# A tuned two-layer hybrid transformer kernel in float32r: 64 bytes of padding behind each of three activation buffers, and 32 bytes ahead of the low weight parts

## The chip, the cores and the metric

The kernel runs on one core of one Trainium2 chip. The metric is the device time of one execution in microseconds. The profile is that of one execution, taken by the hardware profiler; the times beside it are of executions without it.

## The reference, cut to what matters

Two layers over 512 positions of width 1024 are computed in float32: a causal attention with forget gates (16 heads of 64) and a latent attention (16 heads, keys of 128 + 64, values of 128), each followed by a feed-forward block with a causal convolution of width 3, and a last norm.

```python
def conv_ffn(h, w_in, conv_w, conv_b, w_out):
    s_len = h.shape[1]
    u = h @ w_in                                    # 1024 -> 2 x 2816
    up = jnp.pad(u, ((0, 0), (CONV_W - 1, 0), (0, 0)))
    u = conv_b + sum(up[:, j:j + s_len] * conv_w[j] for j in range(CONV_W))
    gate, val = jnp.split(u, 2, axis=-1)
    return (jax.nn.silu(gate) * val) @ w_out        # 2816 -> 1024

def reference(x, ...):
    for layer in range(2):
        if layer < 1:
            x = x + fox_mixer(rmsnorm(x, fox_norm[layer]), ...)
        else:
            k_nope, k_rope, v = mla_shared_kv(x, ...)
            x = x + mla_mixer(rmsnorm(x, mla_norm[0]), ..., k_nope, k_rope, v, cos, sin)
        x = x + conv_ffn(rmsnorm(x, ffn_norm[layer]), ...)
    return rmsnorm(x, final_norm)
```

## The kernel before, in words

Everything is kept transposed: 128 features on the partitions, the 512 positions along the row. To keep float32 accuracy, every operand of a product is split into a high part (rounded to float32r) and a low part (the rest). One product of a weight tile with an activation tile is then three matmuls, written in `mm3`: high weight with high activation (L84), high weight with low activation (L85), low weight with high activation (L86). The weight is the stationary operand of 128 columns, the activation the moving operand of 512 columns. TensorE issues a weight load for every matmul, three per tile of the contraction.

Weights come by one DMA from SP's queue into `raw` (three buffers of 4 KB per partition). `load_w` then lets ScalarE copy them, rounded, into `whi` (L105) and lets VectorE, or POOL in the attention stages, subtract that from `raw` into `wlo` (L106); `whi` and `wlo` have two buffers of 4 KB each.

Activations lie in tiles of the tag `big`: 8 feature tiles, each with 512 high and 512 low values, 32 KB per partition, with three buffers that rotate through the program. `xraw`, `xn`, `oT`, `xs`, `act0`, `act1`, `lat`, the values `V` of the first attention and `qc` of the second all are such tiles. The last 6 feature tiles of the feed-forward's 22 are in `act2`, which lies in the feed-forward's own pool.

In the value projection of the first attention (`mm_v`, L416 to L418) the roles are turned: the activation is the stationary operand, the weight the moving one, with 272, 384 and 384 columns in three passes; one weight tile holds two feature rows `kk`, so that for the first pass row 1 starts 1088 bytes behind row 0. The attention stages have small loops of scores, softmax on ScalarE and VectorE, transposes, and values. In the feed-forward block, `evacuate` multiplies the sum by a norm factor, applies the convolution (L292, L294) and the gate, and splits the result into `act0` to `act2`. Of L294's operands, `c[:, s:]` begins one or two elements into its row.

The pools are laid out one behind the other in each partition, in the order in which they are opened and their tags are first used: small things, `xT` and the four scratch rows `r2`, then `raw`, `whi`, `wlo`, then the three `big`, and behind them the pool of the stage at hand (`fx`, `ffn0`, `ml`, `ffn1`, which share that space in turn). The order of the work is that of the program text; Tile adds the waits.

```python
def mm3(out, w, x, start, stop):
    (wh, wl), (xh, xl) = w, x
    pe.matmul(out, wh, xh, start=start, stop=False)
    pe.matmul(out, wh, xl, start=False, stop=False)
    pe.matmul(out, wl, xh, start=False, stop=stop)
```

Of the kernel before, what the change touches and what calls it, by code (L numbers as in the profile page):

```python
# [7 lines left out]
F32 = mybir.dt.float32  # L8
F32R = mybir.dt.float32r
# [6 lines left out]
P = 128  # L16
S = 512
NT = S // P
# [3 lines left out]
FH, FD = 16, 64  # L22
MH, MN, MR, MV = 16, 128, 64, 128
KVL, QL = 256, 768
KQ = QL // P
KL = KVL // P
# [8 lines left out]
G_FOX, G_FFN, G_KVIN, G_MLA, G_KV, G_Q, G_FIN, G_N = 0, 8, 24, 32, 40, 42, 48, 56  # L35
C_ID, C_MF, C_MM, C_COS, C_SIN, C_U, C_N = 0, 128, 640, 1152, 1664, 2176, 2688
R2 = 4
VCH = (0, 384, 768, 1040)

FOX_FILL = {12: (4, (0,) * 4), 13: ((0, 0, 1, 1), (1,) * 4), 14: ((0, 1, 2, 2), (2,) * 4), 15: ((2,), (3,) * 7)}  # L40
# [6 lines left out]
def tile_kernel(ctx, tc, xT_d, gains_d, bf_d, const_d, conv_d, wv_d, wq_d, wk_d, wfo_d,  # L47
                wdq_d, wdkv_d, wuqn_d, wuqr_d, wuk_d, wuv_d, wmo_d, wfi_d, wfu_d, out_d):
    nc = tc.nc
    v, a, g, pe = nc.vector, nc.scalar, nc.gpsimd, nc.tensor  # L50
# [4 lines left out]
    wp = ctx.enter_context(tc.tile_pool(name="wp", bufs=2))  # L55
    bp = ctx.enter_context(tc.tile_pool(name="bp", bufs=3))
    ps = ctx.enter_context(tc.tile_pool(name="ps", bufs=3, space=PSUM))
    dp = ctx.enter_context(tc.tile_pool(name="dp", bufs=1, space=DRAM))

    cnt = [0]  # L60

    def T(pool, shape, dt, tag, bufs=None):
        cnt[0] += 1
        kw = {} if bufs is None else {"bufs": bufs}
        return pool.tile(shape, dt, tag=tag, name=f"{tag}_{cnt[0]}", **kw)
# [7 lines left out]
    def r2():  # L73
        return T(cp, [P, 512], F32, "r2", R2)

    def big(k, name):
        return T(bp, [P, 8, 2, S], F32R, "big", 3)[:, :k]

    def f(ap):
        return ap.bitcast(F32)  # L80
# [7 lines left out]
    def load_w(src, shape, gain=None, eng=None, into=None, pieces=1):  # L88

        n = 1  # L90
        for s in shape[1:]:
            n *= s
        raw = T(wp, [P, 1024], F32, "raw", 3)[:, :n]
        cuts = [slice(i * n // pieces, (i + 1) * n // pieces) for i in range(pieces)]
        for c in cuts:
            nc.sync.dma_start(raw[:, c], src[:, c])
        if gain is not None:
            k, c = gain
            r3 = raw.rearrange("p (k c) -> p k c", c=n // k)
            g.tensor_tensor(out=r3, in0=r3, in1=c.unsqueeze(2).to_broadcast([P, k, n // k]), op=ALU.mult)  # L100
        if into is None:
            into = T(wp, [P, 1024], F32R, "whi", 2), T(wp, [P, 1024], F32R, "wlo", 2)
        hi, lo = (t[:, :n] for t in into)
        for c in cuts:
            a.copy(hi[:, c], raw[:, c])  # L105
            (eng or v).tensor_tensor(out=lo[:, c], in0=raw[:, c], in1=f(hi[:, c]), op=ALU.subtract)  # L106
        names = " ".join(f"d{i}" for i in range(len(shape) - 1))
        kw = {f"d{i}": shape[i + 1] for i in range(len(shape) - 1)}
        pat = f"p ({names}) -> p {names}"
        return hi.rearrange(pat, **kw), lo.rearrange(pat, **kw)  # L110
# [51 lines left out]
    def bcast_ps(r, m=NT):  # L162
# [6 lines left out]
        for j, part in enumerate((f(rh), rl)):  # L169
            d = T(cp, [P, 512], F32R, "r2", R2)[:, :m * P]  # L170
            for i in range(m):
# [74 lines left out]
    def out_proj(tile_of, gbase):  # L246

        xs = big(KD, "xs")
        squares = Squares()
        for d in range(KD):  # L250
            pt, steps = tile_of(d)
            for _ in steps:
                pass
            v.tensor_tensor(out=xT[:, d, :], in0=pt, in1=xT[:, d, :], op=ALU.add)  # L254
            split_x(xs, d, xT[:, d, :], None if gbase is None else gain(gbase, d))
            squares.add(xT[:, d, :], a if d == KD - 1 else g)
        return xs, squares
# [21 lines left out]
    def ffn(layer, xs, squares, gbase):  # L279
        with tc.tile_pool(name=f"ffn{layer}", bufs=1, reuse_waits="tile") as fp:  # L280
            conv = T(fp, [P, 192], F32, "conv", 1)[:, :KF * 8].rearrange("p (j b c) -> p j b c", b=2, c=4)
            nc.gpsimd.dma_start(conv, conv_d[layer])
            act = [big(8, "act0"), big(8, "act1"), T(fp, [P, KF - 16, 2, S], F32R, "act2", 1)]
            rstd = Rstd(squares)
            cs = {}
# [16 lines left out]
            for j in range(KF):  # L302
                for b in range(2):
                    wh, wl = load_w(wfi_d[layer, j, b], [P, KD, P])
                    pt = acc()
                    for k in range(KD):
                        mm3(pt, (wh[:, k, :], wl[:, k, :]), parts(xs, k), k == 0, k == KD - 1)
                    rstd.after(lambda R, j=j, b=b, pt=pt: evacuate(j, b, pt, R))
# [3 lines left out]
            def load(d, c):  # L312
                k0, kn = chunks[c]
                return load_w(wfu_d[layer, d, :, k0 * P:(k0 + kn) * P], [P, kn, P])
# [76 lines left out]
    with tc.tile_pool(name="fx", bufs=1, reuse_waits="tile") as fp:  # L391
        mask = T(fp, [P, S], F32, "mask", 1)
        bfb = T(fp, [P, 64], F32, "bfb", 1)[:, :FH]
        nc.gpsimd.dma_start(bfb, bf_d)
        xraw = big(KD, "xraw")
        V = T(bp, [P, NT, FH, 2 * FD], F32R, "big", 3)
        squares = Squares()

        def load_v(c, kp):
            if c == 2:  # L400
                nc.sync.dma_start(xT[:, 2 * kp, :], xT_d[2 * kp])
            w = load_w(wv_d[c][kp], [P, 2, VCH[c + 1] - VCH[c]], pieces=2 if (c, kp) == (2, 0) else 1)
            if c == 2:
                nc.sync.dma_start(xT[:, 2 * kp + 1, :], xT_d[2 * kp + 1])
            return w

        def mm_v(c, kp, w, pts):
            n = VCH[c + 1] - VCH[c]
            for kk in range(2):
                k = 2 * kp + kk  # L410
                if c == 2:
                    split_x(xraw, k, xT[:, k, :], gain(G_FOX, k))
                for t in range(NT):
                    xh, xl = parts(xraw, k, slice(t * P, (t + 1) * P))
                    o = pts[t][:, :n]
                    pe.matmul(o, xh, w[0][:, kk, :], start=(k == 0), stop=False)  # L416
                    pe.matmul(o, xh, w[1][:, kk, :], start=False, stop=False)
                    pe.matmul(o, xl, w[0][:, kk, :], start=False, stop=(k == KD - 1))  # L418
            if c == 2:
                for kk in range(2):  # L420
                    squares.add(xT[:, 2 * kp + kk, :], v if kk else a)

        def split_v(c, pts, rs):
            h0, h1 = VCH[c] // FD, min(VCH[c + 1], D) // FD
            for t in range(NT):
                vs = pts[t][:, :(h1 - h0) * FD].rearrange("p (h d) -> p h d", d=FD)
                vh = V[:, t, h0:h1, 0:FD]
                a.activation(vh, vs, AF.Copy, scale=rs[:, t:t + 1])
                v.scalar_tensor_tensor(out=V[:, t, h0:h1, FD:2 * FD], in0=vs, scalar=rs[:, t:t + 1], in1=f(vh),
                                       op0=ALU.mult, op1=ALU.subtract)  # L430

        def forget(pts, rs):
# [3 lines left out]
            for t in range(NT):  # L436
                v.scalar_tensor_tensor(out=z[:, t, :], in0=pts[t][:, D - VCH[2]:VCH[3] - VCH[2]],
                                       scalar=rs[:, t:t + 1], in1=bfb, op0=ALU.mult, op1=ALU.add)
# [112 lines left out]
        def values(h, pT, op_t):  # L551
            e = h % 2
            po = acc()
            for i in range(2):
                for j in range(NT):
                    pe.matmul(po[:, j * P:S], V[:, j, h, :], pT[j][i], start=(i + j == 0), stop=(i == 1 and j == NT - 1))  # L556
            tmp = r2()
# [52 lines left out]
    with tc.tile_pool(name="ml", bufs=1, reuse_waits="tile") as mp:  # L610
# [1 line left out]
        sinT = T(mp, [P, S], F32, "sinT", 1)  # L612
        nc.gpsimd.dma_start(cosT, const_d[:, C_COS:C_COS + S])
        nc.gpsimd.dma_start(sinT, const_d[:, C_SIN:C_SIN + S])
        qc = T(bp, [P, KQ + KL, S], F32, "big", 3)
        rstd = Rstd(squares)

        def down(w_d, gbase, dst):
# [194 lines left out]
def _layout(a):  # L813
# [5 lines left out]
    def cols(w, c0, n):  # L819

        k = w.shape[0] // P
        return np.ascontiguousarray(w[:, c0:c0 + n].reshape(k, P, n).transpose(1, 0, 2)).reshape(P, k * n)

    def tiles(w, n=P):
        return np.stack([cols(w, c, n) for c in range(0, w.shape[1], n)])
# [14 lines left out]
    for c in range(3):  # L840
        n = VCH[c + 1] - VCH[c]
        o[f"wv{c}"] = np.stack([cols(wv[2 * P * k:2 * P * (k + 1)], VCH[c], n) for k in range(KD // 2)])
    o["wq"] = tiles(w[:, :D])
# [37 lines left out]
```

## Time and profile before

| | us |
|---|---|
| median of two runs | 1430.07 (1428.96 to 1431.17) |
| the profiled execution, its own time | 1429.15 |
| its span, first to last instruction | 1427.1 |
| TensorE busy | 1384.2 |
| TensorE weight loads busy | 1162.8 |
| VectorE busy | 902.9 |
| ScalarE busy | 636.5 |
| POOL busy | 310.6 |

The profiled execution has its own time, and the sums below are made against it. Busy time of TensorE counts each matmul from its start to its modelled end; matmuls overlap, so what one costs is read from the starts of its neighbours in the timeline. The granted clock is a share of 2.4 GHz; it is either 1.00 or 0.50, and in between for a stretch that has both.

### The profile page before, as it was taken

What the parts mean: (1) busy time and instruction counts of PE and PEld (TensorE: products, weight loads), DVE (VectorE), ACT (ScalarE), POOL (GpSimd) and SP (SyncE); (2) the same over time, 40 slices, a digit from 0 to 9 for tenths busy, and PEclk for the clock granted to TensorE, in tenths of its full rate; (3) what the DMA queues carried; (4) which work ended last, traced back from release to release, by engine and by line L of the source; (5) the groups of instructions that cost most, each with busy time, mean ns of one, the idle gap of its engine ahead of it and who ended that gap; (6) DMA issues with size and microseconds to landing.
All of it is one profiled execution on the core that took longest, in us unless ns stands there. A gap on an engine that the chain in (4) does not pass through costs nothing.

```text
span 1427.1 us, 17362 instructions
## 1 busy us (share of the span) xinstructions
PE 1384.2 (97%) x6594; PEld 1162.8 (81%) x6594; DVE 902.9 (63%) x1495; ACT 636.5 (45%) x1103; POOL 310.6 (22%) x228
## 2 busy tenths in 40 slices
PE   7999999899999999999799999999999999999997
PEld 7888887788888888888678888888888888888886
DVE  6667786677776744445876666665557777774333
ACT  5588884254444432223454555543225444442111
POOL 4333322400000002154533333321310000000222
PEclk9999999999999999999999999999999999999998
DMA  5321112222323233332111111212232323323331
GB/s 178 102 76 61 51 51 68 89 96 96 103 90 104 89 92 97 106 105 80 50 49 48 59 49 52 61 54 89 89 104 89 104 91 101 98 94 93 96 97 69
DMA packets 41251, 120.22 MB, mean 84 GB/s; under 512 B 5552, under 2 KB 9952, under 8 KB 41168
## 3 DMA queue, kind: packets, MB, share of 16 engines
q1 hardware_dynamic: 39184, 117.00, 25.8%
q0 software_dynamic: 1840, 2.09, 0.6%
q8 instruction: 51, 0.84, 0.2%
q14 instruction: 32, 0.26, 0.1%
q10 hardware_dynamic: 144, 0.03, 0.0%
HBM read 116.74 MB, written 2.36 MB: 83 GB/s over the span
## 4 chain that ended last, share of the span: by engine, by line
PE 85%; DVE 8%; ACT 3%; issue 3%; DMA 1%; POOL 1%; SPq 0%; DVEq 0%; POOLq 0%; ACTq 0%
PE acc L84 24%; PE acc L86 23%; PE acc L85 23%; PE att L208 6%; DVE r L637 2%; PE acc L556 1%; PE att L227 1%; PE acc L709 1%; DVE r L638 1%; DVE ptl L231 1%; DVE big L190 1%; ACT whi L105 1%; DVE tr L667 1%; PE att L84 1%; PE att L86 1%
## 5 line engine op out<-in xcount | busy, mean ns | idle before, releaser
L86 PE MATMUL acc<-big,wlo 128*128 128x512 f32 (+1 forms) x1504 | 584.9, 389 | 7.5 <-POOL wlo L106 3.9
L84 PE MATMUL acc<-big,whi 128*128 128x512 f32 (+1 forms) x1504 | 587.5, 391 | 3.1 <-ACT big L189 2.2
L85 PE MATMUL acc<-big,whi 128*128 128x512 f32 (+1 forms) x1504 | 584.5, 389 | 0.3 <-DVE big L190 0.3
L105 ACT CAST whi<-raw 128x1024 fp32r<-128x1024 f32 (+4 forms) x243 | 229.3, 944 | 427.7 <-PE acc L85 267.5
L86 PEld LDWEIGHTS acc<-big,wlo 128*128 128x128 f32 x1504 | 283.8, 189 | 67.9 <-POOL wlo L106 5.8
L84 PEld LDWEIGHTS acc<-big,whi 128*128 128x128 f32 x1504 | 283.7, 189 | 61.0 <-ACT big L189 2.8
L85 PEld LDWEIGHTS acc<-big,whi 128*128 128x128 f32 x1504 | 283.8, 189 | 58.2 <-DVE big L190 0.6
L106 DVE TENSOR_TENSOR wlo<-raw,whi 128x1024 fp32r<-128x1024 f32 (+3 forms) x179 | 236.2, 1320 | 141.0 <-ACT whi L105 138.3
L142 POOL TENSOR_TENSOR r<-xT 128x512 f32<-128x512 f32 x28 | 31.4, 1124 | 735.9 <-DVE xT L254 414.5
L106 POOL TENSOR_TENSOR wlo<-raw,whi 128x768 fp32r<-128x768 f32 (+3 forms) x64 | 111.8, 1749 | 223.1 <-ACT whi L105 197.3
L294 DVE SCALAR_TENSOR_TENSOR c<-u,conv,c 128x510 f32<-128x510 f32 (+1 forms) x176 | 131.1, 747 | 3.5 <-ACT c L292 0.6
L289 DVE TENSOR_TENSOR u<-acc,R 128x512 f32<-128x512 f32 x88 | 60.3, 687 | 76.3 <-PE acc L86 76.3
L213 ACT ACTIVATE e<-e,nm 128x128 f32<-128x128 f32 (+3 forms) x128 | 71.3, 557 | 43.1 <-DVE nm L211 42.1
L146 POOL TENSOR_TENSOR r<-r,r 128x512 f32<-128x512 f32 x38 | 72.1, 1898 | 27.7 <-ACT r L140 21.0
L292 ACT ACTIVATE c<-u,conv 128x512 f32<-128x512 f32 x88 | 71.4, 813 | 3.1 <-DVE u L289 2.7
L298 ACT ACTIVATE sg<-c 128x512 f32<-128x512 f32 x44 | 27.8, 632 | 78.9 <-DVE c L294 78.8
L231 DVE TENSOR_TENSOR ptl<-att,pth 128x512 fp32r<-128x512 f32 (+3 forms) x128 | 55.4, 481 | 3.4 <-ACT pth L230 2.6
L186 ACT CAST big<-sg 128x512 fp32r<-128x512 f32 x32 | 19.9, 621 | 81.7 <-DVE sg L299 81.6
L230 ACT CAST pth<-att 128x512 fp32r<-128x512 f32 (+3 forms) x128 | 46.9, 435 | 4.8 <-PE att L227 4.3
L208 PE MATMUL att<-kn,tn 128*128 128x128 f32 (+2 forms) x192 | 47.7, 364 | 0.0
L217 DVE TENSOR_SCALAR e<-e,rl 128x128 f32<-128x128 f32 (+3 forms) x128 | 43.0, 399 | 1.1
L254 DVE TENSOR_TENSOR xT<-acc,xT 128x512 f32<-128x512 f32 x20 | 13.8, 691 | 42.5 <-PE acc L86 42.5
(180 smaller groups left out, 1563.8 us busy)
## 6 DMA issues: line engine op xcount, KB each, us to landing
raw<-in_wfi SPq DMA_DIRECT2D x88, 512.0 KB, 3.5
raw<-in_wfu SPq DMA_DIRECT2D x32, 512.0 KB, 3.5
raw<-in_wmo SPq DMA_DIRECT2D x16, 512.0 KB, 3.6
raw<-in_wfu SPq DMA_DIRECT2D x16, 384.0 KB, 3.1
raw<-in_wuqn SPq DMA_DIRECT2D x16, 384.0 KB, 3.0
raw<-in_wq SPq DMA_DIRECT2D x8, 512.0 KB, 3.5
raw<-in_wk SPq DMA_DIRECT2D x8, 512.0 KB, 3.4
raw<-in_wv SPq DMA_DIRECT2D x8, 384.0 KB, 3.1
```

The source lines that it names most:

```text
L84: pe.matmul(out, wh, xh, start=start, stop=False)
L85: pe.matmul(out, wh, xl, start=False, stop=False)
L86: pe.matmul(out, wl, xh, start=False, stop=stop)
L105: a.copy(hi[:, c], raw[:, c])
L106: (eng or v).tensor_tensor(out=lo[:, c], in0=raw[:, c], in1=f(hi[:, c]), op=ALU.subtract)
L146: (adder or g).tensor_tensor(out=self.sum, in0=self.sum, in1=sq, op=ALU.add)
L208: pe.matmul(s_ps[:, :n], lt, rt, start=(j == 0), stop=(j == len(mms) - 1))
L213: a.activation(e, e, AF.Exp, scale=-1.0, bias=nm[:, i:i + 1], accum_out=l[:, i:i + 1])
L231: v.tensor_tensor(out=lo, in0=pt[:, :w], in1=f(hi), op=ALU.subtract)
L289: v.tensor_tensor(out=u, in0=pt, in1=R, op=ALU.mult)
L292: a.activation(c, u, AF.Identity, scale=cw[:, 2:3], bias=cw[:, 3:4])
L294: v.scalar_tensor_tensor(out=c[:, s:], in0=u[:, :S - s], scalar=cw[:, 2 - s:3 - s], in1=c[:, s:], op0=ALU.mult, op1=ALU.add)
```

## The change

The three `big` buffers get 16 more float32 each (64 bytes per partition), in all three places that ask for that tag. Between the first `whi` and the first `wlo` a tile `pad` of 8 float32 (32 bytes) is put, once; a memset by VectorE goes with it.

```diff
+BIGN = 8 * 2 * S + 16
...
     def big(k, name):
-        return T(bp, [P, 8, 2, S], F32R, "big", 3)[:, :k]
+        t = T(bp, [P, BIGN], F32R, "big", 3)
+        return t[:, :8 * 2 * S].rearrange("p (k two s) -> p k two s", two=2, s=S)[:, :k]
...
         if into is None:
-            into = T(wp, [P, 1024], F32R, "whi", 2), T(wp, [P, 1024], F32R, "wlo", 2)
+            whi = T(wp, [P, 1024], F32R, "whi", 2)
+            if not pads:
+                pads.append(T(wp, [P, 8], F32, "pad", 1))
+                v.memset(pads[0], 0.0)
+            into = whi, T(wp, [P, 1024], F32R, "wlo", 2)
...
-        V = T(bp, [P, NT, FH, 2 * FD], F32R, "big", 3)
+        V = T(bp, [P, BIGN], F32R, "big", 3)[:, :8 * 2 * S].rearrange("p (t h d) -> p t h d", h=FH, d=2 * FD)
...
-        qc = T(bp, [P, KQ + KL, S], F32, "big", 3)
+        qc = T(bp, [P, BIGN], F32, "big", 3)[:, :(KQ + KL) * S].rearrange("p (k s) -> p k s", s=S)
```

Where the tiles start, in bytes mod 256, by the addresses in the two built programs:

| tiles | before | after |
|---|---|---|
| `xT`, `r2`, `R`, identity, `raw`, `whi` | 0 | 0 |
| `wlo` | 0 | 32 |
| the three `big` | 0, 0, 0 | 32, 96, 160 |
| tiles of 512 bytes and more in the pools behind them (`act2`, `u`, `c`, `e`, `tn`, `kn`, `tr`, `Vp`, `o`, ...) | 0 | 224 |

How far the moving operand starts from the stationary one, mod 256, counted over the matmuls of 256 columns and more in the two built programs (6013 in each):

| distance | 0 | 32 | 64 | 96 | 128 | 160 | 192 | 224 |
|---|---|---|---|---|---|---|---|---|
| before | 5963 | 0 | 48 | 0 | 1 | 0 | 1 | 0 |
| after | 1273 | 1296 | 872 | 1376 | 201 | 400 | 103 | 492 |

Of the instructions, those of PE, ACT, POOL and SP are the same in the same order, and so are the waits of all engines. On VectorE one is added. This is the start of VectorE's program before; `small`, `ones_r` and `pth` are constants and `big` is the first split activation:

```order
L124 MEMSET small 128x2
L126 MEMSET ones_r 128x128
L127 MEMSET small 128x4
L476 MEMSET pth_9_106 16x512
L190 SCALAR_TENSOR_TENSOR big_89<-xT,gains,big_89 128x512
L106 TENSOR_TENSOR wlo_97<-raw_93,whi_96 128x272
```

And this is the start of VectorE's program now, where the lines of the file lie seven further down:

```order
L131 MEMSET small 128x2
L133 MEMSET ones_r 128x128
L134 MEMSET small 128x4
L108 MEMSET pad_97 128x8
L483 MEMSET pth_10_108 16x512
L197 SCALAR_TENSOR_TENSOR big_89<-xT,gains,big_89 128x512
L113 TENSOR_TENSOR wlo_99<-raw_93,whi_96 128x272
```

The memset of `pad` comes fourth; nothing else has moved.

## Rows read from the trace of the kernel before

**Rows 1.** The page, part 1: busy us (share of the span), instructions.

```profile
span 1427.1 us, 17362 instructions
...
PE 1384.2 (97%) x6594; PEld 1162.8 (81%) x6594; DVE 902.9 (63%) x1495; ACT 636.5 (45%) x1103; POOL 310.6 (22%) x228
```

**Rows 2.** The page, part 4: the chain that ended last.

```profile
PE 85%; DVE 8%; ACT 3%; issue 3%; DMA 1%; POOL 1%; SPq 0%; DVEq 0%; POOLq 0%; ACTq 0%
PE acc L84 24%; PE acc L86 23%; PE acc L85 23%; PE att L208 6%; DVE r L637 2%; PE acc L556 1%; PE att L227 1%; PE acc L709 1%; DVE r L638 1%; DVE ptl L231 1%; DVE big L190 1%; ACT whi L105 1%; DVE tr L667 1%; PE att L84 1%; PE att L86 1%
```

**Rows 3.** Groups by line and shape, mm3: count, busy us, mean ns, idle before.

```profile
L84 PE MATMUL acc<-big,whi 128*128 128x512 f32 x1472 | 578.4, 393 | 3.1 <-ACT big L189 2.2 <-ACT whi L105 0.9
L85 PE MATMUL acc<-big,whi 128*128 128x512 f32 x1472 | 575.4, 391 | 0.3 <-DVE big L190 0.3
L84 PE MATMUL acc<-act,whi 128*128 128x512 f32 x90 | 35.0, 389 | 0.0
```

**Rows 4.** Timeline of PE, first down projection: start us, us, instruction.

```profile
532.96 0.39 PE L84 MATMUL acc<-act,whi 128*128 128x512 f32 x1
...
536.81 0.39 PE L86 MATMUL acc<-act,wlo 128*128 128x512 f32 x1
537.04 0.39 PE L84 MATMUL acc<-big,whi 128*128 128x512 f32 x1
...
541.12 0.39 PE L84 MATMUL acc<-big,whi 128*128 128x512 f32 x1
```

**Rows 5.** Three stretches: length, busy us of PE to POOL, granted clock, DMA.

```profile
13.20:15.60 2.40, 2.40 (x11) 2.40 (x12) 2.40 (x3) 0.62 (x2) 1.02 (x1) 0.50 0.63 216
17.40:23.40 6.00, 6.00 (x50) 6.00 (x49) 5.12 (x5) 3.16 (x5) 3.09 (x3) 1.00 0.39 124
480.00:560.00 80.00, 80.00 (x355) 66.26 (x354) 43.92 (x47) 25.82 (x31) 7.43 (x5) 1.00 0.31 92
```

**Rows 6.** Timeline of the start: VectorE's constants, POOL's first use, the first split.

```profile
0.99 0.06 DVE L127 MEMSET small<- 128x4 f32 x1
1.09 0.48 DVE L476 MEMSET pth<- 16x512 f32 x1
...
3.59 0.54 POOL L478 DMA_DIRECT2D cum_d<-pth  x1
...
4.65 0.75 DVE L190 SCALAR_TENSOR_TENSOR big<-xT,gains,big 128x512 fp32r<-128x512 f32 x1 [3.07 <-ACT big L189]
```

**Rows 7.** Groups by line and shape on VectorE, as in rows 3.

```profile
L294 DVE SCALAR_TENSOR_TENSOR c<-u,conv,c 128x510 f32<-128x510 f32 x88 | 65.8, 749 | 2.9
L294 DVE SCALAR_TENSOR_TENSOR c<-u,conv,c 128x511 f32<-128x511 f32 x88 | 65.5, 746 | 0.6 <-ACT c L292 0.6
L289 DVE TENSOR_TENSOR u<-acc,R 128x512 f32<-128x512 f32 x88 | 60.3, 687 | 76.3 <-PE acc L86 76.3
L190 DVE SCALAR_TENSOR_TENSOR big<-r,gains,big 128x512 fp32r<-128x512 f32 x16 | 11.5, 743 | 1.2 <-ACT big L189 1.2
```

**Rows 8.** Timeline of PE, first value pass, some starts.

```profile
13.53 0.43 PE L418 MATMUL acc<-whi,big 128*128 128x272 f32 x1
...
15.57 0.43 PE L418 MATMUL att<-whi,big 128*128 128x272 f32 x1
...
17.40 0.29 PE L416 MATMUL acc<-whi,big 128*128 128x272 f32 x1
...
18.91 0.29 PE L416 MATMUL acc<-whi,big 128*128 128x272 f32 x1
...
20.43 0.29 PE L416 MATMUL acc<-whi,big 128*128 128x272 f32 x1
...
21.94 0.29 PE L416 MATMUL acc<-whi,big 128*128 128x272 f32 x1
...
23.45 0.33 PE L416 MATMUL acc<-whi,big 128*128 128x384 f32 x1
```

**Rows 9.** The output tile: its transfers and their us from issue to landing.

```profile
L370 SPq DMA_DIRECT2D out_xT<-o x8: 372/381/457, 1415.1 to 1423.5; - x8
...
DMA to landing us min/median/max: 2.1/2.1/2.3
```

More of the change, by code (lines that the diff above doesn't have):

```diff
@@ L60, in tile_kernel @@
     cnt = [0]
+    pads = []
     def T(pool, shape, dt, tag, bufs=None):
```

## The prediction

> **What bounds the kernel now.** I read the page's busy table first, then its chain, then the pitch of the matmuls in the timeline, because a change that only moves buffers can act through nothing but the duration of instructions. TensorE is busy for 1384.2 of 1427.1 us, VectorE for 902.9 and ScalarE for 636.5 [rows 1]. The chain that ended last lies 85% on PE and 8% on VectorE, and the three lines of mm3 (L84, L85, L86) hold 24, 23 and 23% of the span [rows 2]. So the question is what one matmul costs, and whether that cost depends on where its operands start.
>
> The 389 to 393 ns in the groups [rows 3] are latencies of pipelined instructions and overlap; the cost is the distance from one start to the next. In the down projection of the first FFN, from 532.96 to 537.04, 18 matmuls of 512 columns read act2, and from 537.04 to 541.12 another 18 read a big buffer [rows 4]. Either takes 4.08 us, so 226.7 ns each. The granted clock there is 1.00, the 2.4 GHz level [rows 5], where 512 columns take 512/2.4 = 213.3 ns. The remaining 13.3 ns per matmul is all that a better placement of operands could win back.
>
> **The change, part by part.**
>
> *Instruction streams.* The order shows one instruction more, a memset of 128x8 on VectorE behind three other memsets. Every other row and every wait stays. In the trace the memset of 128x4 before that place takes 0.06 us at 0.99, the one behind it 0.48 us at 1.09, and then VectorE sits idle for 3.07 us until ScalarE's first split at 4.65 [rows 6]. I price the new memset as that 0.06 us, hidden in the 3.07 us; uncovered it would cost 0.06 us. POOL's DMAs that read pth come later than 3.5 us and have the same cover. Term: 0.
>
> *Elementwise engines.* In the new kernel most of the pool tiles start 224 B past a multiple of 256, wlo 32 B past, big 32, 96 or 160 B past; r2, xT, raw, whi stay. Does an elementwise instruction cost more for an offset? The trace has one such pair on VectorE. The convolution's scalar_tensor_tensor (L294) reads and writes c one or two elements in, 4 or 8 B past the multiple, while u is read on it: 746 and 749 ns for 511 and 510 elements. The same operation with every operand on the multiple (L190 from r2, both tensors in SBUF) takes 743 ns for 512 [rows 7]. So an offset costs 3 to 6 ns, under 1%. VectorE runs 1495 instructions [rows 1]; at 6 ns each that is 9.0 us of its busy time, and with its 8% of the chain about 0.7 us of the span. ScalarE and POOL show no offset operand; ScalarE's bound from the same row, 1103 x 6 ns x the chain's 3%, is 0.2 us. Below nothing there is a like amount where r2 is read against a shifted tile. I take 0, and keep -1 and +1.
>
> *Matmuls.* The table of distances in the section on the change counts what moves. Before, 5963 of 6013 matmuls of 256 columns or more have moving and stationary start at the same place mod 256. Afterwards 1273 do; 1176 have 64, 128 or 192, and 3564 an odd multiple of 32 (32, 96, 160, 224). The trace of before happens to hold both cases for 64. In the first value pass a weight row of 272 columns is 1088 B long, so for every odd k the moving operand, here whi or wlo, starts 64 B past the stationary, and for every even k at the same place. Groups of twelve matmuls start at 17.40 (k=4, distance 0), 18.91 (k=5, 64), 20.43 (k=6, 0), 21.94 (k=7, 64) and the next pass at 23.45 [rows 8]. That is 1.51, 1.52, 1.51 and 1.51 us: 126 ns each at either distance, against 272/2.4 + 13.3 = 126.7 ns. So 64 instead of 0 changes nothing to within 10 ns in a group, under 1 ns per matmul, and the moving operand's own start 64 B past the multiple is free as well. Larger distances are no different either: act2 starts 768 B behind whi mod 4096, the big buffers 0 B, and both had 226.7 ns [rows 4].
>
> No row shows an odd multiple of 32 on a streaming matmul. Its price is bounded by the extra that a matmul is seen to pay. From below: all of the 13.3 ns goes, 3564 x 13.3 ns = -47.4 us. From above: one more such 13.3 ns comes in, +47.4 us. The value I take is that of the nearest row, distance 64 in the same kernel: 0. If only the split of a run across a boundary cost one column of 1/2.4 = 0.42 ns in all 6013, that would be +2.5 us; I keep it inside the range.
>
> *DMA.* The weights land in raw, which does not move. Of the transfers that do get an offset only the last is on the path: out_xT from o lands 2.1 us after its issue, and its eight issues close the kernel [rows 9]. Constants, masks and the small rows for t2 and m2 are issued far ahead. I take 0 here.
>
> A rule of the Trainium skill speaks against that last zero: "DMA: Bandwidth & Descriptors", section "How a descriptor splits into AXI transactions", says that a transfer is cut at multiples of 256 B and that one which begins off such a multiple fetches bytes it does not use. A row of o is 1024 B from offset 224, so it would take 39 beats in place of 32, 22% more. By that rule at most 22% of the 2.1 us, an estimate of 0.5 us, comes on top; no run here shows it yet.
>
> **Sum.** 0 (memset) + 0 (elementwise) + 0 (matmuls) + 0 (DMA) on the profiled execution's 1429.15 us, of which 1427.1 is the span. That execution lies 0.9 us below the median of two runs, 1430.07 (1428.96 to 1431.17), so I name 1430.0.
>
> **Rivals.**
>
> *Faster: the 13.3 ns are a collision that odd multiples of 32 avoid.* Each matmul loads the next one's weights while its own moving operand streams; were the two to meet at equal starts, a shift could part them. For it: the extra is gone at the 1.2 GHz level. Between 13.53 and 15.57 (granted 0.50 [rows 5]) nine matmuls of 272 columns take 226.7 ns each [rows 8], which is 272/1.2 with nothing over, as one would expect if a slower array left room for both reads. Against it: distance 64 has the full extra, and 272 and 512 columns pay about the same; a plain fixed step between two matmuls at full clock explains that as well. Time: 1429.15 - 47.4 = 1381.8 us. It exceeds 2% (28.6 us) from 2150 matmuls on. The other engines would follow: in the up projection a weight tile takes 24 x 226.7 ns = 5.44 us on PE, and VectorE needs less than that, since it waits 76.3 us there for PE [rows 7].
>
> The Trainium skill gives a smaller extra than I measure: "TensorE: Matmul & The Clock Gate", section "Back-to-back issue gap", has a warm gap of N/2.4 + 2.5 ns. By that figure 10.8 ns are in excess, and 3564 of them are an estimate of 38.6 us, which would end at 1390.5 us. The trace disagrees with the page at distances 0 and 64; whether another distance agrees is what this rival is about.
>
> *Slower: odd multiples of 32 collide.* If reads are organised in pieces of 64 B, the moving operand, whose start is now an odd multiple of 32 in nearly every mm3, needs one piece more than before, and the weights start in another half of a piece than the operand does. One mechanism, in the matmul stream, priced at one more 13.3 ns on 3564 matmuls: 1429.15 + 47.4 = 1476.5 us, and slower by over 2% from 2150 matmuls (or 8.0 ns each) on. Against it: PEld is busy for 1162.8 us with the loads hidden behind PE, and VectorE's 4 and 8 B offsets cost 3 to 6 ns. For it: no row shows a 32 B start.
>
> *The change does not do what it says.* If the allocator rounded the padded sizes up, nothing would move; the built program's addresses do move, as the table shows, so this has next to no weight, and its time is that of the forecast.
>
> **How the numbers follow.** No change 0.87, the faster rival 0.07, the slower 0.06; the slower has a little less, because an unseen extra has to appear where for the faster one a seen extra has only to go. Faster and slower by over 2% (about what a measurement of this kernel can tell from no change) are these same cases, so 0.07, 0.87, 0.06. Within the likeliest, the small bounds are -1 and +1 from elementwise work, +2.5 from a column per split, +0.5 from the tail and +-1.1 from run to run, which makes 1428 to 1435. The rivals hold 0.13 together, so the range needs no whole rival; I widen to 1424 and 1438 for a partial effect at one or two of the eight distances (600 matmuls x 13.3 ns = 8 us).
>
> **What would show it.** Right: the 18 matmuls that read act2 (distances 224 and 192) and the 18 that read a big buffer (32, 96 or 160) still take 4.08 us; the twelves of the first value pass still take 1.51 us; L294 and L190 from r2 keep their means; VectorE's new memset lies before 1.6 us. Wrong: a pitch of 213 to 216 ns (faster) or about 240 ns (slower) that holds for one distance throughout and not for another; or equal pitches with longer VectorE groups, which would put the cost into the attention stages, where the chain passes through VectorE.

## The result and the profile after

The changed kernel takes 1450.35 us (median of two, 1449.76 to 1450.94) against 1430.07 us; the ratio is 1.0142, interval 1.0098 to 1.0185. It is slower by 20 us, outside the forecast range of 1424 to 1438 us. The page of the changed kernel, span and busy times [rows 1] and chain [rows 2]:

```profile
span 1448.9 us, 17363 instructions
...
PE 1408.0 (97%) x6594; PEld 1160.5 (80%) x6594; DVE 904.9 (62%) x1496; ACT 632.8 (44%) x1103; POOL 311.2 (21%) x228
...
PE 84%; DVE 8%; issue 3%; ACT 3%; DMA 1%; POOL 1%; SPq 0%; DVEq 0%; POOLq 0%; ACTq 0%
```

The span grew by 21.8 us and PE's busy time by 23.8, while VectorE's moved by 2.0 and ScalarE's by -3.7 us. The groups on VectorE, as in [rows 7]:

```profile
L301 DVE SCALAR_TENSOR_TENSOR c<-u,conv,c 128x510 f32<-128x510 f32 x88 | 65.9, 750 | 2.9
L301 DVE SCALAR_TENSOR_TENSOR c<-u,conv,c 128x511 f32<-128x511 f32 x88 | 65.4, 744 | 0.6 <-ACT c L299 0.6
L197 DVE SCALAR_TENSOR_TENSOR big<-r,gains,big 128x512 fp32r<-128x512 f32 x16 | 11.5, 743 | 1.2 <-ACT big L196 1.2
```

All within 2 ns of before. What changed is the distance between the starts of matmuls. The timeline of PE in the first down projection, as [rows 4]:

```profile
537.80 0.39 PE L87 MATMUL acc<-big,whi 128*128 128x512 f32 x1
...
541.30 0.40 PE L87 MATMUL acc<-act,whi 128*128 128x512 f32 x1
...
545.47 0.39 PE L87 MATMUL acc<-big,whi 128*128 128x512 f32 x1
```

Fifteen matmuls that read a big buffer take 3.50 us, 233.3 ns each; eighteen that read act2 take 4.17 us, 231.7 ns each. Both were 226.7. The first value pass, as [rows 8], has distances of 32 and 224 in it now (beside 0 and 64) and has not become slower:

```profile
17.55 0.29 PE L423 MATMUL acc<-whi,big 128*128 128x272 f32 x1
...
19.04 0.29 PE L423 MATMUL acc<-whi,big 128*128 128x272 f32 x1
...
20.54 0.29 PE L423 MATMUL acc<-whi,big 128*128 128x272 f32 x1
...
22.05 0.29 PE L423 MATMUL acc<-whi,big 128*128 128x272 f32 x1
```

Twelve matmuls of 272 columns take 1.49 to 1.51 us, where they took 1.51 and 1.52.

Where the 21.8 us lie is seen from the factor's multiplication in the feed-forward (L289, now L296), whose first and last start bracket the up projection. Line queries of before and then of the changed kernel, for the first layer and the second:

```profile
L289 DVE TENSOR_TENSOR u<-acc,R x44: 681/686/692, 280.4 to 507.3; 128x512 f32<-128x512 f32 x44
...
L289 DVE TENSOR_TENSOR u<-acc,R x44: 681/684/692, 1066.5 to 1293.4; 128x512 f32<-128x512 f32 x44
```

```profile
L296 DVE TENSOR_TENSOR u<-acc,R x44: 679/691/693, 281.4 to 515.0; 128x512 f32<-128x512 f32 x44
...
L296 DVE TENSOR_TENSOR u<-acc,R x44: 678/692/694, 1078.9 to 1312.6; 128x512 f32<-128x512 f32 x44
```

All that comes before the first layer's feed-forward costs 1.0 us more; one up projection, 43 tiles of 24 matmuls, costs 233.6 in place of 226.9 us, 6.7 more. The second layer's takes 233.7, also in place of 226.9. So the two up projections hold 13.5 of the 21.8 us.

### The profile page after: what moved, and what is told of

Read it like the earlier page. It is cut to its first block, busy times and chain, and to the rows that moved or that the text cites. A ratio compares the mean times of both kernels' runs of the same rounds, so it can differ in the third digit from the quotient of the medians.

```text
span 1448.9 us, 17363 instructions
## 1 busy us (share of the span) xinstructions
PE 1408.0 (97%) x6594; PEld 1160.5 (80%) x6594; DVE 904.9 (62%) x1496; ACT 632.8 (44%) x1103; POOL 311.2 (21%) x228
## 4 chain that ended last, share of the span: by engine, by line
PE 84%; DVE 8%; issue 3%; ACT 3%; DMA 1%; POOL 1%; SPq 0%; DVEq 0%; POOLq 0%; ACTq 0%
PE acc L87 24%; PE acc L88 23%; PE acc L89 23%; PE att L215 6%; DVE r L644 2%; PE acc L563 1%; PE att L234 1%; PE acc L716 1%; DVE r L645 1%; DVE ptl L238 1%; DVE big L197 1%; ACT whi L112 1%; PE att L87 1%; DVE tr L674 1%; PE att L89 1%
## 5 line engine op out<-in xcount | busy, mean ns | idle before, releaser
L89 PE MATMUL acc<-big,wlo 128*128 128x512 f32 (+1 forms) x1504 | 592.3, 394 | 7.3 <-POOL wlo L113 3.8
L87 PE MATMUL acc<-big,whi 128*128 128x512 f32 (+1 forms) x1504 | 594.9, 396 | 3.0 <-ACT big L196 2.2
L88 PE MATMUL acc<-big,whi 128*128 128x512 f32 (+1 forms) x1504 | 592.3, 394 | 0.1
L296 DVE TENSOR_TENSOR u<-acc,R 128x512 f32<-128x512 f32 x88 | 60.6, 691 | 83.2 <-PE acc L89 83.1
```

Source lines behind the costliest of these rows:

```text
L296: v.tensor_tensor(out=u, in0=pt, in1=R, op=ALU.mult)
```

## The experiments

Two theories stood against my forecast at first, that a moving operand pays for its own start (START) or for its distance from the weights (DISTANCE), and a third, that weights at two starts in turn pay (MIX).

**One part alone, and all starts shifted together.** `big_only` leaves the 32 bytes ahead of wlo out, `wlo_only` leaves the padding of the buffers out, `all_32` is `wlo_only` with the pad one tile earlier:

```diff
-            whi = T(wp, [P, 1024], F32R, "whi", 2)
             if not pads:
                 pads.append(T(wp, [P, 8], F32, "pad", 1))
                 v.memset(pads[0], 0.0)
+            whi = T(wp, [P, 1024], F32R, "whi", 2)
```

Expected of `big_only`:

> Only the three padded buffers, without the 32 bytes ahead of wlo: all starts and distances are multiples of 64 (whi and wlo 0, big 0, 64, 128, the pools 192). START, DISTANCE and MIX all expect 1430 us, as before, with a pitch of 226.7 ns. If any distance other than 0 costs, it stays near 1450 for the buffers at 64 and 128.

Of `wlo_only`:

> Only the 32 bytes ahead of wlo: whi 0, wlo, big and all pools 32. START: all moving operands of mm3 start at 32, so 1450 us or a little more, pitch 233.3 ns on all three lines. DISTANCE: 32 against whi, 0 against wlo, so two of three matmuls pay: 226.7 + 6.7 x 2/3 = 231 ns, 1445 us. MIX: 1450 us.

Of `all_32`:

> The 32 bytes go ahead of whi instead: whi, wlo, big and all pools start at 32, so every distance of mm3 is 0 again while every start is an odd multiple of 32. START: 1450 us, pitch 233.3 ns. DISTANCE and MIX: 1430 us, pitch 226.7 ns.

Measured: `all_32` 1431.11 us, ratio 1.0004 (0.9991 to 1.0017); `wlo_only` 1451.6 us, 1.0157 (1.0140 to 1.0174); `big_only` 1438.46 us, 1.0065 (1.0050 to 1.0080). One tile of the first up projection, 24 matmuls, in the timelines of `all_32`, `wlo_only` and `big_only`:

```profile
399.85 0.39 PE L87 MATMUL acc<-big,whi 128*128 128x512 f32 x1
...
405.29 0.39 PE L87 MATMUL acc<-big,whi 128*128 128x512 f32 x1
```

```profile
399.73 0.40 PE L87 MATMUL acc<-big,whi 128*128 128x512 f32 x1
...
405.33 0.40 PE L87 MATMUL acc<-big,whi 128*128 128x512 f32 x1
```

```profile
399.96 0.39 PE L87 MATMUL acc<-big,whi 128*128 128x512 f32 x1
...
405.46 0.39 PE L87 MATMUL acc<-big,whi 128*128 128x512 f32 x1
```

5.44 us (226.7 ns each) with every operand at 32; 5.60 us (233.3) with the activation 32 bytes past whi; 5.50 us (229.2) with it 64 bytes past. START falls, since `all_32` has nothing but odd starts and pays nothing; it also clears the memset and the shift of every later tile. DISTANCE had 231 ns and 1445 us for `wlo_only`, and missed: 233.3 ns and 1451.6 us. A distance of 64 does cost at 512 columns, against all three theories as I had priced them and against my reading of the trace.

A further control, `pad_256`, was to put 256 bytes ahead of wlo, so that every later tile moves and every start mod 256 stays as before; 1430 us was expected. It gave no time: the pool of the latent attention needs 56.25 KB per partition, and 56.22 would have been left. What it asked is answered in part by `all_32`, in which every later tile moves by 32 bytes.

**A map of the placements.** The kernel runs matmuls back to back, for each placement 36 that step through four activation and eight weight tiles:

```python
m0 = ms[j % len(ms)] // 4 + 512 * (j % 4)
s0 = ss[j % len(ss)] // 4 + 128 * (j % 8)
pe.matmul(pt[:, :n], st[:, s0:s0 + 128], mv[:, m0:m0 + n], start=(j == 0), stop=(j == 35))
```

> This kernel does none of the model: it copies x to the output and runs 36 matmuls in a row for each of 114 placements of the operands (moving and stationary start in steps of 32 bytes mod 256 at 512 columns; 256, 384 and 128 columns for eight moving starts; the mm3 pattern with stationary starts 0, 0, 32; finer and coarser steps). START theory (a moving operand that starts at an odd multiple of 32 bytes needs one more 64-byte piece, 16 columns, 6.7 ns): 233.3 ns in all rows of the grid with an odd moving start whatever the stationary start, 226.7 in the others; the same 6.7 ns at 256 and 384 columns. DISTANCE theory (a collision of the two reads that depends on their difference mod 256 alone): 233.3 ns along the diagonals with an odd difference, 226.7 at a difference of 0 and of 64. MIX theory (the cost comes from weights that lie at two different starts in turn, hi at 0 and lo at 32): 226.7 in the whole grid, 233.3 only in the mm3 pattern. My forecast of before, no dependence at all: 226.7 everywhere, and the rise in the changed kernel would have another cause.

Mean ns from start to start at 512 columns, worked out from the starts in its trace, first four matmuls of each placement left out (rows: moving start mod 256, columns: weights' start):

```
        0     32     64     96    128    160    192    224
  0  226.9  233.2  233.4  234.2  232.7  233.2  229.0  233.1
 32  233.3  227.3  233.2  233.4  234.2  232.7  233.2  229.0
 64  229.0  233.3  226.9  233.2  233.3  234.2  232.7  233.2
 96  233.5  229.0  233.1  226.9  233.2  233.4  234.2  232.7
128  232.7  233.2  229.0  233.1  226.9  233.2  233.3  234.2
160  234.2  232.7  233.2  229.0  233.1  226.9  233.2  233.3
192  233.3  234.2  232.7  233.2  229.0  233.1  226.9  233.2
224  233.1  233.4  234.2  232.7  233.2  228.9  233.1  226.9
```

Each diagonal has one value to within 0.5 ns: between multiples of 32 the difference alone decides, and only 0 is free. Distances of 256, 512 and 1024 give 227.4, 226.7 and 226.9. MIX is not needed for a cost, though weights at 0, 0 and 32 in turn with the activation at 32 take 233.2 rather than the 231.3 that is the mean of their cells; `wlo_only` has the same 233.3.

**Columns, and pairs.** The second map takes the moving start in steps of 4 bytes and then fewer columns.

> Again none of the model: x goes to the output, and each placement of the operands gets 36 matmuls in a row, under a name of its own in the trace (a letter for the kind, then two letters for the moving start in units of 16 bytes and of 1 byte). First the moving start in steps of 4 bytes at 512 columns, stationary at 0. If whole pieces of 32 or 64 bytes collide, the pitch is a staircase with steps of that width and equal to the first map at its eight points (226.9, 233.1, 229.0, 233.3, 232.7, 234.2, 233.4, 233.2); if single words collide, neighbours of 0 (4 and 252) already pay about 6 ns or more, and 0 is a narrow valley. FIXED-STEP theory: 13.3 ns belong to the change of weights, so no distance gets below 226.7 at 512 columns. HIDDEN-COLLISION theory: part of the 13.3 ns is a collision too, so some distance lies below 226.7, down to 215. Second, the eight distances at 256, 272, 320, 384, 448 and 480 columns: if the first value pass misled me because the effect needs long rows, 272 columns show 126 to 127 ns at 0 and at 64 alike, and the gap between the two opens towards 512. Third, weights and rows that alternate between two starts (32, 96 or 160 apart): OWN theory (a matmul collides with its own weights) expects 226.7 for own and about 233 for next; NEXT theory (it collides with the load of the following weights, which runs beside it) the reverse. Last, weights of 64 and 32 columns: if the extra grows with the length of the load, 64 columns take about 220 ns at distance 0.

A row of its timeline holds a placement; (duration - last matmul) / 35 is the pitch. At 512 columns with distances 0, 32, 64, 128; then 256 columns at 0 and 192, 272 at 0 and 64, 320 at 0 and 64:

```profile
38.23 8.32 PE L61 MATMUL daa<-mv,st 128*128 128x512 f32 x36
...
105.27 8.56 PE L61 MATMUL dca<-mv,st 128*128 128x512 f32 x36
...
172.48 8.42 PE L61 MATMUL dea<-mv,st 128*128 128x512 f32 x36
...
307.46 8.56 PE L61 MATMUL dia<-mv,st 128*128 128x512 f32 x36
...
577.36 4.47 PE L61 MATMUL paa<-mv,st 128*128 128x256 f32 x36
...
602.97 4.28 PE L61 MATMUL pma<-mv,st 128*128 128x256 f32 x36
...
611.33 4.67 PE L61 MATMUL qaa<-mv,st 128*128 128x272 f32 x36
...
620.37 4.72 PE L61 MATMUL qea<-mv,st 128*128 128x272 f32 x36
...
647.46 5.44 PE L61 MATMUL raa<-mv,st 128*128 128x320 f32 x36
...
658.01 5.44 PE L61 MATMUL rea<-mv,st 128*128 128x320 f32 x36
```

That is 226.6, 233.4, 229.4 and 233.4 ns at 512 columns, with a last matmul of 0.39 us; at 256 columns 0 is not the best (120.0 against 113.5 from the starts); 272 columns differ by 1.4 ns and 320 by nothing. So the value pass, with 272 columns, could not show what 512 columns pay. Of 64 distances in steps of 4 bytes none lies below 226.7 at 512 columns; starts at 4 and 20 past a multiple of 32 reach 236 to 240, except 148 with 233.3. OWN and NEXT both fail: with starts 32 apart 231.8 and 233.1, 96 apart 233.9 and 229.9, 160 apart 233.8 and 230.3. Weights of 64 and 32 columns take 229.7 and 231.5, so the 13.3 ns do not shrink with the load.

**Looking for less than 226.7.**

> Looks for a pitch under 226.7 ns at 512 columns; nothing of the model is computed, x goes to the output. 36 matmuls per placement: weights read with a step of 2, 4, 8 or 16 words (each against eight moving starts), weights of eight tiles interleaved word by word, activations read with a step of 2, weight steps of 3, 5, 7, 9 and 65 words, the same weights or the same activations every time, weights or activations that advance by 32 or 128 bytes more from matmul to matmul, and 256 columns with a weight step of 8. FIXED-STEP theory: 13.3 ns per matmul belong to the change of weights, the floor stays at 226.7 and only extras come and go. HIDDEN-COLLISION theory (the 113.5 ns of 256 columns at a distance of 192 in the second map, 6.8 ns over 256/2.4, speak for it): the two reads still meet at distance 0, and some placement that spreads the weight read over other pieces lies clearly below, 216 to 222 ns. If one does, it is worth 5 to 10 ns on some 4,500 matmuls, 20 to 45 us of the kernel.

Timeline rows: weights with a step of 2 words, of 8 words, activations with a step of 2, the same weights and activation every time, weights advancing by 32 bytes more per matmul:

```profile
37.10 8.56 PE L68 MATMUL fbaa<-mv,st 128*128 128x512 f32 x36
...
172.30 8.97 PE L68 MATMUL fhaa<-mv,st 128*128 128x512 f32 x36
...
381.47 16.52 PE L68 MATMUL mbaa<-mv,st 128*128 128x512 f32 x36
...
571.35 8.32 PE L68 MATMUL sameboth<-mv,st 128*128 128x512 f32 x36
...
579.51 8.57 PE L68 MATMUL advst<-mv,st 128*128 128x512 f32 x36
```

From the starts: 233.3, 244.5, 453.3, 226.7 and 233.8 ns. Nothing lies below 226.7 at 512 columns; FIXED-STEP is not refuted there, and the kernel of before already runs on that floor; nor is it shown, since the same weights every time cost the 13.3 ns too. At 256 columns it fails: 113.5 ns is less than 256/2.4 + 13.3 = 120.0.

**Does the map foretell a kernel?** Both halves of a split weight in one tile with 8 words to spare, begun 7 or 1 words in:

```diff
-            into = T(wp, [P, 1024], F32R, "whi", 2), T(wp, [P, 1024], F32R, "wlo", 2)
+            both = T(wp, [P, 2056], F32R, "whi", 2)
+            into = both[:, 7:7 + 1024], both[:, 7 + 1024:7 + 2048]
```

Expected of `start_28`:

> A test of the map on placements that nobody chose for a reason. The kernel of before, with whi and wlo halves of one tile of 2056 words in two buffers, and both begun 7 words into it. The buffers then put the big tiles 36 bytes past the weights from one tile and 4 bytes past those from the other (2388 and 2346 matmuls of 512 columns). The second map has 239.6 and 236.9 ns there, 12.9 and 10.2 over 226.7: 2388 x 12.9 + 2346 x 10.2 = 54.7 us at most, and about nine tenths of such a sum came through so far, so 1476 to 1484 us and a pitch that changes from weight tile to weight tile between 239.6 and 236.9. If the map holds only for the rows it was made with, or only odd multiples of 32 matter, 1430 to 1450.

Of `start_4`, which has 1 for 7:

> The same program as start_28 with the same tiles, begun 1 word into them instead of 7, so 24 bytes earlier: distances of 60 and 28 bytes. The second map has 229.2 and 230.0 ns, 2.5 and 3.3 over 226.7: 2388 x 2.5 + 2346 x 3.3 = 13.7 us at most, so 1441 to 1444 us. The joint tile and its waits are the same in both, so the difference between the two kernels, 41 us by the map, is of the placement alone; a theory without distances expects none.

Measured: 1446.89 us (1.0122, 1.0097 to 1.0147) and 1439.77 us (1.0066, 1.0041 to 1.0091). The order of the two is as foretold, the sizes are not: 7 us apart instead of 41. In the starts of their traces the matmuls have 233.3 and 232.9 ns at distances 36 and 4, and 233.2 and 230.9 at 60 and 28. So `start_28` missed in pitch and in time, and `start_4` came close by luck: its matmuls pay more than foretold (2388 x 6.5 + 2346 x 4.2 = 25 us), and less of it arrives. In `start_28`, 2388 x 6.6 + 2346 x 6.2 = 30 us became 16.5 us. The nine tenths assumed above are not what the runs until then show either: in `wlo_only` 4734 x 6.6 = 31 us became 22. Where the rest goes is told in the section on why the prediction was wrong.

`v_192` begins the weights of the latent attention's value projection 48 words into whi and wlo:

> The only gain that the maps offer: 113.5 ns at 256 columns and a distance of 192, against 120.0 at 0. The kernel of before with the weights of the latent attention's value projection begun 192 bytes into whi and wlo: 192 matmuls of 256 columns, 6.5 ns each, 1.2 us at most if they were all on the chain. Expected 1428 to 1430 us, not to be told from before, and a pitch of 113 to 115 ns in that line.

It took 1428.86 us, ratio 0.9998 (0.9985 to 1.0011): not to be told from before. The pitch fell from 119.8 to 117.8 ns, not to 113.5; why was not tested.

**Which operand is off the multiple of 32.** The last map moves the weights instead of the activation, then repeats some placements in the order of mm3.

> start_28 and start_4 came out at pitches that the second map does not have for their distances: 233.3 and 232.9 ns at 36 and 4 bytes (map 239.6 and 236.9), 233.2 and 230.9 at 60 and 28 (map 229.2 and 230.0). In the map it was the moving operand that began off a multiple of 32, in those kernels the weights. Nothing of the model again; 48 matmuls of 512 columns per placement. First the weights' start in steps of 4 bytes with the moving operand at 0. SIDE theory (a moving operand off a multiple of 32 has a cost of its own, and weights have not): no value above 234.5, and about 233, 233, 233 and 231 ns at weight starts of 220, 252, 196 and 228. Then the same with the order of mm3 (high weights twice, low weights once, the two halves of the activation in turn). ORDER theory (the sequence of addresses decides): the simple order repeats the second map's 237 to 240 ns at the mirrored starts, and only the order of mm3 gives 231 to 233. The eight multiples of 32 should repeat the first map in both. Last, the order of mm3 with the moving operand at 4, 36, 28 and 60: SIDE expects some 237, 240, 230 and 229 ns, ORDER 231 to 233.

Timeline rows with 48 matmuls each, order of mm3: weights at 220, 252, 196 and 228 (activation at 0), then the activation at 4, 36, 28 and 60 (weights at 0):

```profile
845.87 11.36 PE L65 MATMUL tnm<-mv,st 128*128 128x512 f32 x48
857.06 11.36 PE L65 MATMUL tpm<-mv,st 128*128 128x512 f32 x48
868.26 11.36 PE L65 MATMUL tme<-mv,st 128*128 128x512 f32 x48
879.46 11.23 PE L65 MATMUL toe<-mv,st 128*128 128x512 f32 x48
890.53 11.59 PE L65 MATMUL xae<-mv,st 128*128 128x512 f32 x48
901.95 11.47 PE L65 MATMUL xce<-mv,st 128*128 128x512 f32 x48
913.26 11.16 PE L65 MATMUL xbm<-mv,st 128*128 128x512 f32 x48
924.26 11.15 PE L65 MATMUL xdm<-mv,st 128*128 128x512 f32 x48
```

From the starts, first six left out: 233.3, 233.3, 233.2 and 230.5 ns, the values of `start_28` and `start_4` within 0.5; then 238.2, 235.6, 228.9 and 228.9, where the second map has 236.9, 239.6, 230.0 and 229.2. The eight multiples of 32 repeat the first map within 1 ns. So off a multiple of 32 it matters which operand is moved: the activation at 4 and 36 takes 236 to 240 ns in either order, the weights at the mirrored starts 252 and 220 at most 233.3. ORDER falls, since the simple order does not repeat the second map either.

SIDE is borne out in the order of mm3 and only in part in the simple order: the weights at 220 and 196 take 233.1 and 233.2 ns, but at 252 and 228 226.8, where it had 233 and 231. Starts of 120, 132, 144, 156 and 240 come down to 226.8 to 228.4 as well, and seven starts lie above its ceiling of 234.5, up to 237.1. So off the multiples of 32 the sequence of addresses has a part too, and the maps give no rule there.

## Why the prediction was wrong

*What bounds the kernel*, the pitch of the matmuls, was the right place to look, and nothing else was seen to add time: the memset takes 0.07 us and stays hidden, VectorE's groups hold, `all_32` has the same memset and moves every later tile for nothing, and the transfers of the output, now off a multiple of 256, land after 2.2 in place of 2.1 us. An estimate from "DMA: Bandwidth & Descriptors", section "How a descriptor splits into AXI transactions", of the Trainium skill had put that at 0.5 us at most; the trace has 0.1.

*The step that failed* is the value of the matmul term: "So 64 instead of 0 changes nothing to within 10 ns in a group, under 1 ns per matmul", and from it "The value I take is that of the nearest row, distance 64 in the same kernel: 0". The observation was sound and is repeated by the second map: at 272 columns 0 and 64 are alike to 1.4 ns. It was carried to 512 columns, where 64 costs 2.3 ns and the distances that the change makes cost more. I treated the 13.3 ns, equal at 272 and 512 columns, as a sign that rows of either length behave alike off 0; they do only at 0. A second leap, from 64 to odd multiples of 32, rested on no row, as the prediction says.

The measured term, by the starts of three consecutive mm3 matmuls in the changed kernel and by the first map's rows with weights at 0, 0, 32:

```
start of the activation      32     96    160    224
changed kernel, ns         233.2  233.3  231.5  231.6
first map, ns              233.2  233.4  231.5  231.3
```

Against 226.7 that is 4.8 to 6.6 ns on some 4,700 matmuls. Summed over some 4,600 pairs of neighbouring mm3 matmuls of 512 columns at full clock, from start to start, the changed trace has 26.3 us more than that of before; the term was put at 0. The up projections, which are PE from end to end at a granted clock of 1.00, paid it in full (2 x 43 x 24 x 6.6 ns = 13.6 us, 13.5 measured).

*What took some of it back* was the granted clock, which no term of the prediction had. Each kernel spends some stretches at the half level of 1.2 GHz. There 512 columns have a pitch of 427 ns, as eight matmuls show in the timeline of PE before, just after PE had waited 3.54 us for wlo:

```profile
254.57 0.63 PE L84 MATMUL acc<-big,whi 128*128 128x512 f32 x1
...
257.99 0.56 PE L86 MATMUL acc<-big,wlo 128*128 128x512 f32 x1
```

So a microsecond at the half level loses 1 - 226.7/427 = 0.47 us where TensorE is the bound. How long it lasted follows from the mean granted clock of the span, here before and then in the changed kernel:

```profile
core 0: 1427.1 us, clock 0.983
```

```profile
core 0: 1448.9 us, clock 0.987
```

That is 2 x 0.017 x 1427.1 = 48.5 us at the half level before and 37.7 after, worth 5 us. The same estimate for the other kernels, as differences from before, in us:

| kernel | added by the starts | granted clock | at the half level | added, less 0.47 x (48.5 - half level) | span measured |
|---|---|---|---|---|---|
| changed | 26.3 | 0.987 | 37.7 | 21.2 | 21.8 |
| `all_32` | 0.0 | 0.982 | 51.4 | 1.4 | 2.0 |
| `wlo_only` | 27.7 | 0.986 | 40.6 | 24.0 | 24.3 |
| `big_only` | 8.8 | 0.983 | 48.8 | 8.9 | 9.6 |
| `start_28` | 26.6 | 0.991 | 26.0 | 16.0 | 18.0 |
| `start_4` | 21.9 | 0.992 | 23.0 | 9.9 | 11.6 |

The two together come within 2 us of the span in all six. Why the clock stays up longer in some kernels is not shown. That only 1.0 us arrived ahead of the first feed-forward has one cause that the traces show: in both kernels the clock falls about that wait of 3.5 us, and from 250 to 260 us it is granted 0.66 before and 0.83 in the changed kernel. The other engines, through which the first attention's chain passes too, may hide more; that was not tested.

*The rivals.* The faster one is excluded at 512 columns: no placement tried went below 226.7. The slower one had the place right, the matmul stream, at half of the price for the changed kernel's worst distance (6.6 instead of 13.3 ns) and with the wrong condition: not odd multiples of 32 and not pieces of 64 bytes, but, at 512 columns, every multiple of 32 that is not one of 256. That its point from which it decides was set at 8.0 ns on 3564 matmuls left out what happened, 5 to 7 ns on 4,700, which is 1.4% and between the cases. At 1.4% it falls to the case of no change within 2%, to which I gave 0.87, but by where the line was drawn and not by the reason that I gave. My widening for a partial effect, 8 us, was sized for one or two distances; all of the eight but 0 paid.

*What stays open* is the mechanism. At multiples of 32 equal differences give equal pitches, which speaks for the two reads of TensorE acting on each other, but no run looks inside; whether a matmul meets its own weights or those loaded beside it was not told apart, nor why 320 columns are free and 256 columns run best at 192, nor why the half level of the clock lasts less in some kernels. The Trainium skill ("TensorE: Matmul & The Clock Gate", section "Step-by-step: what each phase is for") has two independent read ports, so that loading the next weights takes no bandwidth from the running matmul. The runs differ: at 512 columns the placement of the weights against the activation changes the pitch by up to 7.5 ns at multiples of 32 and by 13 off them.

No version beat the kernel of before; `v_192`, the only gain that the maps offered, was within the noise.

## What to carry to other kernels

In a kernel that is bound by float32r matmuls of 512 columns, keep the moving and the stationary operand at the same start mod 256 bytes: tiles with sizes that are multiples of 256 do that by themselves, and 32 bytes ahead of one of them cost 1.6% here, 64 bytes behind each of three buffers 0.65%. When a sum over matmuls and a time disagree, compare the granted clocks before looking for something that hides the rest. A control inside the old trace is worth only as much as its shape is like that of the case: repeat it at the size that carries the time. And where an unseen cost has bounds of 47 us on either side, a range of 14 us claims that a part of it cannot happen; ask what excludes the middle.

## What the runs showed of the hardware that was not expected

- At 512 columns the pitch has a floor of 226.7 ns (512/2.4 + 13.3) that nothing tried could break, reached at a distance of 0, with the same operands every time alike, and with weights at some starts off a multiple of 32 (120, 132, 144, 156, 228 and 252 in the last map).
- An activation read with a step of two words doubles the pitch, 453.3 ns; weights with a step of 2 words cost 6.6 ns and with a step of 8 words 17.8 ns, and at 256 columns a step of 8 words takes 240 to 244 ns.
- With fewer columns distance 0 is not always the best: at 480 columns the best of the eight distances is 128 (213.3 ns against 216.7 at 0), at 448 it is 64 (200.0 against 202.6), at 256 it is 192; at 384 distance 0 shares the lowest value, and at 320 and 128 all eight are alike.
- `start_28` and `start_4` were granted 0.991 and 0.992 of the clock where the kernel of before had 0.983. The pitch alone does not decide this: `wlo_only` has the same 233 ns as `start_28`, and 0.986.
